# More unread products ahead of TensorE's waits in the two feed-forward layers and in retention's input projections

## The chip, the cores and the metric

The kernel runs on one core of a Trainium2 chip, in one launch. The metric is the device time of one execution in microseconds (us). All arithmetic on the matrices is fp32, with each large product split into three products of rounded fp32 parts (high times high, high times low, low times high), which TensorE takes as `fp32r`, one instruction each. A product of plain fp32 operands stands in the trace as two instructions.

The engines are named as in the profile: PE is TensorE, PEld its loading of weights, DVE VectorE, ACT ScalarE, POOL GpSimd and SP the queue that issues most transfers. Each engine takes its instructions in the order in which the program holds them.

## The reference, cut to what matters

A trunk of two layers works on one sequence of 1024 rows by 1024 columns. Layer 0 mixes with a gated delta rule, layer 1 with retention; each is followed by a convolutional feed-forward network.

```python
for i in range(DEPTH):
    mod = (e @ ada_w[i] + ada_b[i])[:, None, :]
    sh1, sc1, g1, sh2, sc2, g2 = jnp.split(mod, 6, axis=-1)
    y = mixers[i % N_MIXERS](x * (1.0 + sc1) + sh1)
    x = layer_norm(DN_ALPHA * x + (1.0 + g1) * y, ln_g[i, 0], ln_b[i, 0])
    y = conv_ffn(x * (1.0 + sc2) + sh2, ffn_up[i], ffn_conv_w[i], ffn_conv_b[i], ffn_down[i])
    x = layer_norm(DN_ALPHA * x + (1.0 + g2) * y, ln_g[i, 1], ln_b[i, 1])
```

The parts that the change touches are products: the feed-forward network's up projection (1024 to 2 x 2816) and down projection (2816 to 1024), and retention's input projection (1024 to 6144).

```python
gate, up = jnp.split(h @ w_up, 2, axis=-1)          # conv_ffn
return (jax.nn.silu(causal_dwconv(gate, conv_w) + conv_b) * up) @ w_down
q, k, v, gate = jnp.split(h @ w_in, [...], axis=-1)  # retention
```

## The kernel before, in words

**Up projections and retention's input projection** are done by `strassen(...)`. It goes over a list of items; each is two units of 128 output columns. The first two items are plain products. From the third on (`n` = 2, 3, ...) an item is one call of `wino`, a Winograd scheme on a 2 x 2 split: seven block products in place of eight. DVE first adds and subtracts weight blocks (`psub`), ACT and DVE split each sum into a high and a low part (`block`, line 1219 on, whose two instructions are lines 89 and 90), and PE multiplies (`prod`, four times three products, lines 110 to 112; where the product adds to a bank that is in use it goes by `mm_on`, line 1175). In `wino` the products come in the order 11, 12, T1, T2, 22, T3, T4. The product T2 needs the block `w2`, which is the last of a chain on DVE and ACT: `s1`, `s2`, its rounding, its rest.

`strassen` is called three times: for layer 0's feed-forward network, for retention's input projection (with `direct=True`), and for layer 1's feed-forward network.

**Down projections** are done by `proj_gen(...)`, also a Winograd scheme: seven products `p` = 0 to 6, each summed over `nj` pairs of inner blocks (`j`), 11 for the feed-forward network, with four banks of 128 x 512. For each `j`, `ops` loads and splits an activation block (`ab`) and a weight block (`bb`), and PE makes 12 products of 128 x 512 (line 1500). The functions `f1` to `f7` read the banks as each `p` ends. In `p` = 2, two of the four banks come from the pool `sc`, which has two buffers, and two from `acc`, which has four; in `p` = 3 the two `acc` banks come first and the two of `sc` after. `p` = 6 adds to the banks of `p` = 5 after `f7` (line 1475) has read each. `gate` is set for retention's output projection alone, `final` for layer 1's feed-forward network alone.

**Unread products.** `keep_busy(n, mm, behind)` takes a bank from `sc` and issues `n` fp32 products of the identity with 384 columns of constants into it; nothing reads them (line 686). They wait for the bank alone. The kernel before has them at seven places in the code (some through `pm`, which stand in the profile under line 633). Two of these are in `wino` for `n` = 2 without `direct`: three ahead of T1 and three ahead of T2.

**What sets the order.** The instructions are written down in program order, and a scheduler with a model of time then orders each engine's list; `tc.issue_after(x)` keeps an instruction behind `x` in that order. A tile of a pool that is full waits until an older tile of the pool is no longer used, so a bank of `sc` that is asked for while both buffers hold sums cannot be written before one of them was read, wherever it stands in the code.

Of the kernel before, what the change touches and what calls it, by code (L numbers as in the profile page):

```python
# [33 lines left out]
def trunk_kernel(ctx: ExitStack, tc, A):  # L34
    nc = tc.nc
    pe, act, dve, pool, sp = nc.tensor, nc.scalar, nc.vector, nc.gpsimd, nc.sync
# [9 lines left out]
    def tl(tag, shape, dt=F32, name=None):  # L46
        return sb.tile(shape, dt, tag=tag, name=name or tag, bufs=BUFS[tag])
# [10 lines left out]
    def acc_tile():  # L58
        return ps.tile([P, HALF], F32, tag="acc", name="acc", bufs=4)
# [4 lines left out]
    def sc_tile():  # L64
        return ps.tile([P, HALF], F32, tag="sc", name="sc", bufs=2)

    def acc4():
        return [acc_tile(), acc_tile(), acc_tile(), acc_tile()]
# [13 lines left out]
    def hs(half):  # L82
        return slice(half * HALF, (half + 1) * HALF)
# [30 lines left out]
    ended = [None]  # L114
# [509 lines left out]
    def pq(inst, cost):  # L624
        if pin[0] is not None:
            tc.add_manual_dep(inst.ins, pin[0].name,
                              mybir.DependencyInfo(mybir.DependencyClass.NoSync, mybir.DependencyReason.DATA),
                              reason="issue order")
        pin[0] = inst.ins
        clk[0] += cost  # L630

    def pm(out, lhsT, rhs, start=True, stop=True, cost=0.216, **kw):
        r = pe.matmul(out, lhsT, rhs, start=start, stop=stop, **kw)  # L633
        pq(r, cost)
        return r
# [46 lines left out]
    def keep_busy(n, mm, behind=None):  # L682
        t = sc_tile()
        with tc.issue_after(behind) if behind is not None else nullcontext():
            for _ in range(n):
                mm(t[:, 0:3 * P], ident, cst)
# [9 lines left out]
    def take(tag, n):  # L696
        while free[tag] < n:
            yield lambda: free[tag] >= n
        free[tag] -= n

    def give(tag, n):
        free[tag] += n
# [465 lines left out]
    def strassen(hT0, xts, scale, shift, items, tags=("hTb", "hTb", "qkv", "qkv", "aux"), direct=False, beside=None, spare="lane"):  # L1168
# [35 lines left out]
        def bg_steps(n):  # L1204
            for _ in range(0 if n < 4 else 2 if n < 8 else 1):
                bg_step()

        def block(src, it):
            n = nblk[0]
            nblk[0] += 1  # L1210
            t = tl(("wh", "wl")[n % 2], [P, 2, HALF], F32R, name="wb")
            with rank(it):
                split(t[:, 0], t[:, 1], src)
            return kn(t[:, 0]), kn(t[:, 1])

        def prod(it, src, b, onto=None, w=None):
            w = w or block(src, it)
            if onto is None:
                nacc[0] += 1
                acc = (acc_tile, acc_tile, sc_tile)[nacc[0] % 3]()  # L1220
            else:
                acc = onto
            for k in range(4):
                mm3(acc, w, k, B[b][k], onto is None and k == 0, k == 3, mm_on if onto is not None else pe.matmul)
            return acc

        def psub(it, x, y, op=ALU.subtract):
            t = mm_tile()
            with rank(it):
                dve.tensor_tensor(t, x, y, op)  # L1230
            return t

        def wino(n, sink):
            ua, ub = items[n][:2]
            raws = []
            for m, u in ((2 * n, ua), (2 * n + 1, ub)):
                if direct and m % 3 == 0:
                    raws += [tl("xT", [P, HALF], name="wr") for _ in range(2)]
                    for h2 in range(2):
                        anchor["i"] = sp.dma_start(raws[-2 + h2], u[:, hs(h2)])  # L1240
                else:
                    w = tl("wr", [P, D])
                    anchor["i"] = sp.dma_start(w, u)
                    raws += [w[:, hs(0)], w[:, hs(1)]]
            if beside:
                beside(n)
            a11, a12, a21, a22 = raws
            def copy_of(X, tag="cv"):
                t = tl(tag, [P, 516] if tag == "cv" else [P, HALF], name="pc")[:, 0:HALF]
                act.activation(t, X, AF.Copy)  # L1250
                return t

            X = prod(n, a11, "11")
            p1 = copy_of(X)
            s1 = psub(n, a21, a22, ALU.add)
            sink(0, prod(n, a12, "21"), p1)
            s2 = psub(n, s1, a11)
            w1 = block(s1, n)
            if n == 2 and not direct:
                keep_busy(3, pe.matmul, ended[0].ins)  # L1260
            Z = prod(n, None, "T1", w=w1)
            z5 = copy_of(Z)
            s4 = psub(n, a12, s2)
            w2 = block(s2, n)
            if n == 2 and not direct:
                keep_busy(3, pe.matmul, ended[0].ins)
            prod(n, None, "T2", X, w=w2)
            u2 = copy_of(X)
            s3 = psub(n, a11, a21)
            prod(n, s4, "22", Z)  # L1270
            sink(1, Z, u2)
            bg_steps(n)
            prod(n, s3, "T3", X)
            u3 = copy_of(X, "t2")
            sink(3, X, z5)
            sink(2, prod(n, a22, "T4"), u3)
            bg_steps(n if n < 4 else 8)
# [29 lines left out]
    def proj_gen(nj, ablk, wsrc, slots, xsrc, G, final, ln_next, tag, ltags, dst, key, mm=pe.matmul, gate=None, gain=None):  # L1307
# [137 lines left out]
        def finish(half, t, nh, c):  # L1445
            add_row(stats[half][t], nh, xts[half][t][:, hs(nh)], c)
# [51 lines left out]
        for p, (an, bn, fin) in enumerate(prods):  # L1498
            onto = p in (1, 5, 6)
            mm_ = (lambda *a, p=p, onto=onto, **kw: (mm if p < 2 else pe.matmul)(*a, skip_group_check=onto, **kw))  # L1500
            if p in (2, 3):
                accs = [sc_tile(), sc_tile(), acc_tile(), acc_tile()] if p == 2 else [acc_tile(), acc_tile(), sc_tile(), sc_tile()]
            elif not onto:
                accs = acc4()
            tail = []
            depth = ltags[3] if p == 6 else 2
            for j in range(nj):
                if gate and p < 2:
                    yield gate(j)
                    yield from take("qkv", 2)  # L1510
                    give("qkv", 2)
                a, w = ops(p * nj + j)
                ops_ahead(p * nj + j + 1)
                if gate and p == 0 and j == 0:
                    keep_busy(3, lambda *x: pm(*x, cost=0.0))
                if gain and p == 0 and j < 8:
                    gain_half(j)
                if gain and p == 1 and j % 2 == 0 and j < 8:
                    xload(0, j // 2)
                if gate and p == 2 and j < 4:  # L1520
                    xload(0, j)
                if not gate and not gain and p == 2 and j % 2 == 0 and j < 8:
                    xload(0, j // 2)
                if p == 3 and j < 4:
                    finish(0, j, 0, c11[j])
                if j >= nj - depth:
                    tail.append((j, a, w))
                else:
                    for t in range(4):
                        mma(accs[t], t, a, w, j == 0 and not onto, False, mm_)  # L1530
                        yield 0.0
                for _ in range(3 if p == 5 else 1):
                    if later:
                        later.pop(0)()
                if p == 5 and not later:
                    for _ in range(-(-16 // (nj - 4))):
                        if hooks:
                            hooks.pop(0)()
                bg_step()
            while later:  # L1540
                later.pop(0)()
            if p == 5:
                while hooks:
                    hooks.pop(0)()
            if p == 6:
                pin[0] = None
            if p == 6 and final:
                keep_busy(2, pe.matmul, ended[0].ins)
            for t in range(4):
                for j, a, w in tail:  # L1550
                    mma(accs[t], t, a, w, j == 0 and not onto, j == nj - 1,
                        (lambda *x, **kw: pm(*x, skip_group_check=True, **kw)) if p == 6 else mm_)
                fin(t, accs[t])
                yield 0.0
            if p == 1:
                yield "P2"
            if p == 4:
                hooks = [] if final else ln_hooks(0, xts[0], tag, ln_next, outs, dst, key, bal["h"])
                hooks += [lambda t=t: xload(1, t) for t in range(4)]
# [472 lines left out]
```

## Time and profile before

| | |
|---|---|
| time, median of 3 runs | 2918.78 us (2918.34 to 2925.48) |
| the profiled execution | 2926.89 us |
| its span, first to last instruction | 2925.1 us |
| mean granted TensorE clock | 0.994 |
| unread products by line 686 / all instructions of PE | 17 (34 records) / 13718 |

The span is one execution, and it is 6.3 us longer than the median of the three runs. All places below are in us from the start of this span. In the timeline, a row gives the start, the length from the first start to the last end, the engine, line, operation, tiles, shape and count, and in brackets how long the engine had been idle and what ended that. The lengths of PE's instructions overlap, since they are pipelined. The table of stretches gives the busy time of each engine, then `PEclk`, the granted share of TensorE's clock, then the share of the transfer engines and GB/s.

### The profile page before, as it was taken

What the parts mean: (1) busy time and instruction counts of PE and PEld (TensorE: products, weight loads), DVE (VectorE), ACT (ScalarE), POOL (GpSimd) and SP (SyncE); (2) the same over time, 40 slices, a digit from 0 to 9 for tenths busy, and PEclk for the clock granted to TensorE, in tenths of its full rate; (3) what the DMA queues carried; (4) which work ended last, traced back from release to release, by engine and by line L of the source; (5) the groups of instructions that cost most, each with busy time, mean ns of one, the idle gap of its engine ahead of it and who ended that gap; (6) DMA issues with size and microseconds to landing.
All of it is one profiled execution on the core that took longest, in us unless ns stands there. A gap on an engine that the chain in (4) does not pass through costs nothing. (4 is left out here: it accounts for less than half of the span.)

```text
span 2925.1 us, 39004 instructions
## 1 busy us (share of the span) xinstructions
PE 2825.9 (97%) x13718; PEld 2303.7 (79%) x13718; DVE 2204.2 (75%) x3965; ACT 1315.2 (45%) x2457; POOL 423.4 (14%) x485
## 2 busy tenths in 40 slices
PE   8999999999999999999999999999999999999997
PEld 7787877887778878887787877777778788888786
DVE  6695687557788888997687766566797887778878
ACT  3755465443544444536443332221345544444443
POOL 0311220134011111000000000323301011111001
PEclk9999999999999999999999999999999999999999
DMA  8122221354344544863435454555574243335753
GB/s 304 69 80 80 98 91 44 105 189 142 105 155 162 165 159 147 313 220 123 159 108 175 147 186 147 160 158 176 185 243 152 70 164 108 108 108 206 261 155 119
DMA packets 239236, 442.37 MB, mean 151 GB/s; under 512 B 22848, under 2 KB 76352, under 8 KB 239040
## 3 DMA queue, kind: packets, MB, share of 16 engines
q1 hardware_dynamic: 206832, 387.96, 40.1%
q10 hardware_dynamic: 29760, 43.00, 4.0%
q0 software_dynamic: 2448, 8.91, 0.8%
q8 instruction: 108, 1.77, 0.3%
q14 instruction: 88, 0.72, 0.1%
HBM read 331.26 MB, written 108.53 MB: 150 GB/s over the span
## 5 line engine op out<-in xcount | busy, mean ns | idle before, releaser
L1500 PE MATMUL acc<-bb,ab 128*128 128x512 f32 x1800 | 426.0, 392 | 6.5 <-DVE pa L1475 3.3
L1500 PEld LDWEIGHTS acc<-bb,ab 128*128 128x128 f32 x1800 | 337.3, 188 | 80.1 <-issue 3.7
L633 PE MATMUL acc<-hT,wh 128*128 128x512 f32 x960 | 299.8, 394 | 0.0
L1643 POOL TENSOR_TENSOR o<-o 128x512 f32<-128x512 f32 x88 | 121.1, 1385 | 803.1 <-DVE o L1636 753.7
L1175 PE MATMUL acc<-T,wb 128*128 128x512 f32 x840 | 203.0, 391 | 8.1 <-DVE wb L90 7.9
L633 PEld LDWEIGHTS acc<-hT,wh 128*128 128x128 f32 x960 | 182.6, 190 | 34.0
L89 ACT ACTIVATE ab<-ar 128x512 fp32r<-128x512 f32 x210 | 128.7, 623 | 176.0 <-PE acc L1500 72.2
L633 PE MATMUL acc<-hT,wl 128*128 128x512 f32 x480 | 202.4, 422 | 0.8 <-DVE qkv L1008 0.4
L1175 PEld LDWEIGHTS acc<-T,wb 128*128 128x128 f32 x840 | 157.0, 188 | 44.5 <-DVE wb L90 12.2
L90 DVE TENSOR_TENSOR ab<-ar,ab 128x512 fp32r<-128x512 f32 x210 | 147.2, 709 | 42.1 <-ACT ab L89 39.3
L90 DVE TENSOR_TENSOR wb<-mm,wb 128x512 fp32r<-128x512 f32 x216 | 145.4, 686 | 26.8 <-ACT wb L89 25.0
L90 DVE TENSOR_TENSOR wb<-wr,wb 128x512 fp32r<-128x512 f32 x162 | 112.4, 695 | 65.4 <-ACT wb L89 64.7
L89 ACT ACTIVATE wb<-mm 128x512 fp32r<-128x512 f32 x216 | 122.6, 594 | 82.7 <-DVE mm L1230 74.7
L89 ACT ACTIVATE wh<-wr 128x1024 fp32r<-128x1024 f32 x101 | 107.0, 1061 | 116.5 <-PE acc L633 56.0
L90 DVE TENSOR_TENSOR wl<-wr,wh 128x1024 fp32r<-128x1024 f32 x85 | 105.5, 1241 | 62.8 <-ACT wh L89 60.7
L1250 ACT ACTIVATE pc<-acc 128x512 f32<-128x512 f32 x143 | 84.7, 592 | 149.9 <-PE acc L1175 90.8
L89 ACT ACTIVATE wb<-wr 128x512 fp32r<-128x512 f32 x162 | 98.9, 626 | 102.9 <-DMA wr<-in_ffn_up 53.3
L1622 DVE SCALAR_TENSOR_TENSOR o<-g,vc,o 128x512 f32<-128x512 f32 (+2 forms) x176 | 139.1, 808 | 1.5 <-ACT o L1617 0.9
L633 PE MATMUL acc<-wh,hT 128*128 128x512 f32 x384 | 137.0, 419 | 3.2 <-DVE vv L90 3.2
L452 DVE SCALAR_TENSOR_TENSOR qkv<-raw,vc,qkv 128x512 f32<-128x512 f32 x144 | 112.3, 783 | 31.2 <-ACT qkv L450 27.2
L224 DVE SCALAR_TENSOR_TENSOR ada<-mvw,e,ada 128x512 f32<-128x512 f32 x140 | 105.9, 757 | 24.5 <-DMA mvw<-in_ada_w 23.9
L1230 DVE TENSOR_TENSOR mm<-wr 128x512 f32<-128x512 f32 x108 | 79.0, 731 | 53.3 <-DMA wr<-in_ffn_up 30.9
(630 smaller groups left out, 6955.5 us busy)
## 6 DMA issues: line engine op xcount, KB each, us to landing
wr<-in_ffn_up SPq DMA_DIRECT2D x96, 512.0 KB, 4.1
ad<-o SPq DMA_DIRECT2D x154, 256.0 KB, 3.0
ar<-ad SPq DMA_DIRECT2D x154, 256.0 KB, 4.0
mvw<-in_ada_w SPq DMA_DIRECT2D x48, 512.0 KB, 5.2
Br<-in_ffn_down SPq DMA_DIRECT2D x66, 256.0 KB, 3.5
mvw<-in_ada_w SPq DMA_DIRECT2D x64, 256.0 KB, 3.0
wr<-in_ret_wv SPq DMA_DIRECT2D x32, 512.0 KB, 3.7
ar<-od SPq DMA_DIRECT2D x56, 256.0 KB, 5.3
```

Source lines behind the costliest of these rows:

```text
L89: act.activation(dst_h, src, AF.Copy)
L90: eng.tensor_tensor(dst_l, src, dst_h, ALU.subtract)
L224: dve.scalar_tensor_tensor(a, wr[kk], e[:, k:k + 1], a, ALU.mult, ALU.add)
L452: dve.scalar_tensor_tensor(oh, raw[:, 3 - j:515 - j], w[:, 3 - j:4 - j], oh, ALU.mult, ALU.add)
L633: r = pe.matmul(out, lhsT, rhs, start=start, stop=stop, **kw)
L1175: return pe.matmul(*a, skip_group_check=True, **kw)
L1230: dve.tensor_tensor(t, x, y, op)
L1250: act.activation(t, X, AF.Copy)
L1500: mm_ = (lambda *a, p=p, onto=onto, **kw: (mm if p < 2 else pe.matmul)(*a, skip_group_check=onto, **kw))
L1622: dve.scalar_tensor_tensor(tv, gv[:, c0 - j:c1 - j], w[:, 2 - j:3 - j], tv, ALU.mult, ALU.add)
L1643: pool.tensor_tensor(o[d], o[x], o[y], op)
```

## The change

It alters the number of unread products at one place and adds them at three more:

- `wino`, `n` = 2 without `direct` (once in each feed-forward layer), ahead of T2: nine in place of three;
- `wino`, `n` = 4 with `direct` (retention's input projection), ahead of T2: eight, where there were none;
- `proj_gen`, `final`, `p` = 6, `j` = 0 (layer 1's down projection): eight, where there were none;
- `proj_gen` without `gate`, `p` = 2, `j` = 1 (the down projection of both layers): five, where there were none.

That is 38 products of 128 x 384 more, 76 records of PE. No arithmetic that is read changes.

```diff
             if n == 2 and not direct:
-                keep_busy(3, pe.matmul, ended[0].ins)
+                keep_busy(9, pe.matmul, ended[0].ins)
+            if n == 4 and direct:
+                keep_busy(8, pe.matmul, ended[0].ins)
             prod(n, None, "T2", X, w=w2)
...
                 if gate and p == 0 and j == 0:
                     keep_busy(3, lambda *x: pm(*x, cost=0.0))
+                if final and p == 6 and j == 0:
+                    keep_busy(8, pe.matmul, ended[0].ins)
+                if p == 2 and j == 1 and not gate:
+                    keep_busy(5, pe.matmul, ended[0].ins)
```

The order on PE at three places follows. In each, the rows before stand first. `cst` holds the constants, `wb` a split weight block of `wino`, `T_` a block of the activations, `bb` and `ab` the split blocks of `proj_gen`.

Place A, PE in layer 0's up projection, third item: the last product of T1, then T2. Layer 1 has the same.

```order
L112 MATMUL acc<-T_7318,wb 128x512
L686 MATMUL sc<-cst 128x384 x3
L1175 MATMUL acc<-T_7242,wb 128x512 x3
L1175 MATMUL acc<-T_7266,wb 128x512 x3
L1175 MATMUL acc<-T_7290,wb 128x512 x3
L1175 MATMUL acc<-T_7314,wb 128x512 x3
```

```order
L112 MATMUL acc<-T_7318,wb 128x512
L686 MATMUL sc<-cst 128x384 x9
L1175 MATMUL acc<-T_7242,wb 128x512 x3
L1175 MATMUL acc<-T_7266,wb 128x512 x3
L1175 MATMUL acc<-T_7290,wb 128x512 x3
L1175 MATMUL acc<-T_7314,wb 128x512 x3
```

The count alone differs. In retention's input projection the eight new ones stand in the same way between T1 and T2 of the fifth item (place C below).

Place B, PE in layer 0's down projection, with buffer numbers: before, banks 11600 to 11603 are those of `p` = 3, and 11329 to 11332 those of `p` = 2; in the change they are 11612 to 11615 and 11335 to 11338.

```order
L1500 MATMUL acc_11600<-bb_11681,ab_11678 128x512 x3
L1500 MATMUL acc_11601<-bb_11681,ab_11678 128x512 x3
L1500 MATMUL sc_11602<-bb_11566,ab_11563 128x512 [waits DVE_49]
L1500 MATMUL sc_11602<-bb_11566,ab_11563 128x512 x2
L1500 MATMUL sc_11602<-bb_11609,ab_11606 128x512 x3
```

```order
L1502 MATMUL acc_11612<-bb_11693,ab_11690 128x512 x3
L1502 MATMUL acc_11613<-bb_11693,ab_11690 128x512 x3
L686 MATMUL sc_11375<-cst_155 128x384 [waits DVE_49]
L686 MATMUL sc_11375<-cst_155 128x384 x4
L1502 MATMUL sc_11614<-bb_11578,ab_11575 128x512 [waits DVE_49]
L1502 MATMUL sc_11614<-bb_11578,ab_11575 128x512 x2
```

The five products do not stand at `p` = 2, `j` = 1, where the code has them, but after five `j` of `p` = 3 in the `acc` banks and ahead of its first product in an `sc` bank; in layer 1 after four `j`. Between the rows of `j` = 0 and `j` = 1 of `p` = 2 there is nothing new.

Place D, PE in layer 1's down projection, the end of the program:

```order
L1500 MATMUL acc<-bb,ab 128x512 x12
L1500 MATMUL sc<-bb,ab 128x512 x12
L1500 MATMUL acc<-bb,ab 128x512 x324
L686 MATMUL sc<-cst 128x384 x2
L633 MATMUL acc<-bb,ab 128x512 x72
```

```order
L1502 MATMUL acc<-bb,ab 128x512 x12
L1502 MATMUL sc<-bb,ab 128x512 x12
L1502 MATMUL acc<-bb,ab 128x512 x264
L686 MATMUL sc<-cst 128x384 x8
L1502 MATMUL acc<-bb,ab 128x512 x60
L686 MATMUL sc<-cst 128x384 x2
L633 MATMUL acc<-bb,ab 128x512 x72
```

The eight stand ahead of the last 60 products by line 1500, which are the first five `j` of `p` = 6.

On DVE and ACT the scheduler moves single instructions by a few rows near places A, B and C, and near D a split of `ab` goes between two additions of rows; POOL and SP keep their order.

## The prediction

> **What bounds the kernel now.** I read the page first: it says which engine is full.
>
> ```profile
> span 2925.1 us, 39004 instructions
> PE 2825.9 (97%) x13718; PEld 2303.7 (79%) x13718; DVE 2204.2 (75%) x3965; ACT 1315.2 (45%) x2457; POOL 423.4 (14%) x485
> PEclk9999999999999999999999999999999999999999
> ```
>
> PE is busy for 97% of the span, so time that is added to PE's list is added to the span unless it lies in one of PE's own waits. PEclk never shows less than a nine, so little clock is to be won. Next I read PE's timeline for its waits, and stretches of the granted clock around each. The clock changes on a grid of 3.41 us, so I chose stretches of that length on its edges.
>
> The price of one unread product comes from the three ahead of T2 in layer 0 (place A) and the group of line 686.
>
> ```profile
> L686 PE MATMUL sc<-cst x34: 483/486/488, 640.2 to 2894.5; 128*128 128x384 f32 x34
> 806.93 2.10 PE L686 MATMUL sc<-cst 128*128 128x384 f32 x6
> 811.06 3.02 PE L1175 MATMUL acc<-T,wb 128*128 128x512 f32 x12 [2.04 <-DVE wb L90]
> 2312.13 2.10 PE L686 MATMUL sc<-cst 128*128 128x384 f32 x6
> 2316.31 3.02 PE L1175 MATMUL acc<-T,wb 128*128 128x512 f32 x12 [2.08 <-DVE wb L90]
> ```
>
> Six records take 2.10 us and each is 0.486 long, so they start (2.10 - 0.486) / 5 = 0.323 us apart; a product is two records, 0.646 us. The next could start 0.323 after the last start, while the record runs on for 0.486: a wait offers its shown idle time and 0.16 more as room.
>
> **The change part by part.** For each place: products times 0.646, less the room, is the delay; then the clock.
>
> *Place A, twice.* Six more products are 3.88 us. The room is 2.04 + 0.16 = 2.20 and 2.08 + 0.16 = 2.24. The delays are 1.68 and 1.64, together 3.32 us. What PE waited for, the last split of `wb` on DVE, does not depend on the products, so it comes when it came. The clock before was full here (the stretches are below), so this execution has nothing to win back.
>
> *Place B, twice.* The code puts five products at `p` = 2, `j` = 1, where PE waits 1.75 and 1.69 us:
>
> ```profile
> 1259.85 1.65 PE L1500 MATMUL sc<-bb,ab 128*128 128x512 f32 x6 [1.75 <-DVE ab L90]
> 2757.86 1.67 PE L1500 MATMUL sc<-bb,ab 128*128 128x512 f32 x6 [1.69 <-DVE ab L90]
> ```
>
> But both buffers of `sc` hold sums of `p` = 2 then, so PE's order has them some 35 us later, ahead of the first `sc` products of `p` = 3. There the trace has:
>
> ```profile
> 1288.77 5.38 PE L1500 MATMUL acc<-bb,ab 128*128 128x512 f32 x23
> 1293.98 6.96 PE L1500 MATMUL sc<-bb,ab 128*128 128x512 f32 x30
> 2782.52 8.32 PE L1500 MATMUL acc<-bb,ab 128*128 128x512 f32 x36
> 2790.68 5.60 PE L1500 MATMUL sc<-bb,ab 128*128 128x512 f32 x24
> 1289.79 0.72 DVE L1463 TENSOR_TENSOR pa<-sc,pa 128x512 f32<-128x512 f32 x1
> 1291.59 0.72 DVE L1463 TENSOR_TENSOR pa<-sc,pa 128x512 f32<-128x512 f32 x1
> ```
>
> No wait stands ahead of either row of `sc` products: there is no room, and 2 x 5 x 0.646 = 6.46 us go on top. The banks' readers on DVE (line 1463) had ended by 1292.31, ahead of 1293.98, so the bank itself costs no further wait. The old waits of 1.75 and 1.69 stay. Could the delay be swallowed, because DVE sets the pace? DVE is full up to here, but then has slack:
>
> ```profile
> 1304.00:1314.00 10.00, 10.00 (x46) 8.29 (x45) 6.21 (x11) 4.32 (x8) 0.00 (x0) 1.00 0.67 225
> 2802.00:2812.00 10.00, 10.00 (x46) 8.27 (x45) 6.16 (x11) 4.38 (x8) 0.00 (x0) 1.00 0.73 241
> ```
>
> The third number is DVE's busy time: 6.2 of 10 us, with PE at 10 of 10. PE sets the pace, so I take the whole 6.46; the bounds are 0 (swallowed) and 6.46 + 1 (the scheduler moved line 1463's reads by a row on a full DVE, and one instruction there takes 0.72).
>
> *Place C, once.* Eight products are 5.17 us in retention's fifth item.
>
> ```profile
> 1554.26 0.39 PE L112 MATMUL acc<-T,wb 128*128 128x512 f32 x1
> 1557.68 5.49 PE L1175 MATMUL sc<-T,wb 128*128 128x512 f32 x12 [3.03 <-DVE wb L90]
> 1562.97 1.25 PE L1175 MATMUL acc<-22_12947,wb 128*128 128x512 f32 x3
> 1564.75 0.84 PE L1175 MATMUL acc<-22_12987,wb 128*128 128x512 f32 x3
> 1553.58:1556.99 3.41, 1.07 (x5) 0.56 (x3) 3.41 (x7) 2.61 (x5) 0.00 (x0) 1.00 0.22 77
> 1556.99:1560.40 3.41, 2.72 (x6) 2.17 (x7) 3.41 (x7) 0.10 (x1) 1.39 (x2) 0.50 0.60 231
> 1560.40:1563.82 3.42, 3.42 (x10) 2.67 (x8) 0.93 (x2) 1.21 (x3) 0.04 (x1) 0.50 0.91 226
> ```
>
> The room is 3.03 + 0.16 = 3.19, so the delay is 1.98. Here the clock paid: after a stretch in which PE was busy for 1.07 of 3.41 us, two stretches ran at 0.50. Twelve products took 5.49 against 3.02 in the row at 811.06, and three took 1.25 against 0.84: 2.47 + 0.41 = 2.88 us, which go if PE never idles. Net -0.90.
>
> *Place D, once.* Eight products are 5.17 us at the start of `p` = 6 in layer 1.
>
> ```profile
> 2739.70 13.76 PE L1500 MATMUL acc<-bb,ab 128*128 128x512 f32 x60
> 2878.50 15.21 PE L1500 MATMUL acc<-bb,ab 128*128 128x512 f32 x60 [3.34 <-DVE pa L1475]
> 2879.58 1.30 DVE L1475 TENSOR_TENSOR pa<-acc,pa 128x512 f32<-128x512 f32 x2
> 2874.54:2877.95 3.41, 0.62 (x3) 0.19 (x1) 3.41 (x8) 1.65 (x3) 0.93 (x1) 1.00 0.00 0
> 2877.95:2881.37 3.42, 2.87 (x7) 2.32 (x8) 3.42 (x7) 0.00 (x0) 0.36 (x1) 0.50 0.40 153
> ```
>
> The room is 3.34 + 0.16 = 3.50 and the delay 1.67. The half clock up to 2881.37 made 60 products take 15.21 where 60 elsewhere take 13.76: 1.45 us come back. The next two banks are read by 2880.88, before PE would now reach them. Net +0.22. What follows to the end is a chain on DVE behind PE's last products, and shifts with them.
>
> *Given back.* PE that comes later may find a later wait for DVE shorter. After places A these are left:
>
> ```profile
> 1026.77 3.01 PE L1175 MATMUL acc<-T,wb 128*128 128x512 f32 x12 [0.59 <-DVE wb L90]
> 2336.14 2.12 PE L1175 MATMUL sc<-T,wb 128*128 128x512 f32 x8 [0.49 <-DVE wb L90]
> 2400.37 0.50 PE L110 MATMUL sc<-T,wb 128*128 128x512 f32 x1 [0.47 <-DVE wb L90]
> ```
>
> Together 1.55 us at most, nothing at least, since DVE there also waits for PE's banks; I take 0.6.
>
> *The sum.* Delays 3.32 + 6.46 + 1.98 + 1.67 = 13.43; clock 2.88 + 1.45 = 4.33; given back 0.6: +8.5 us. The profiled execution took 2926.89 us (a span of 2925.1 and 1.8 around it), so it would take 2935.4. It lies 8.1 above the median of the runs; the profile doesn't show why, so I add the difference, not a ratio, to the median: 2918.78 + 8.5 = 2927.3 us. A measurement of this kernel can tell about 0.3% from no change, which is 8.8 us: the forecast lies on that edge.
>
> *A rule against the trace.* How long must a wait be to cost clock?
>
> ```profile
> 1990.37 1.57 PE L633 MATMUL sc<-vv,kz 128*128 128x512 f32 x3 [2.08 <-DVE on L1862]
> 1987.08:1990.49 3.41, 1.33 (x7) 0.79 (x6) 3.25 (x6) 0.00 (x0) 1.46 (x1) 1.00 0.84 241
> 1990.49:1993.90 3.41, 3.41 (x14) 3.13 (x15) 2.43 (x4) 0.47 (x1) 0.00 (x0) 0.50 0.97 333
> 2311.32:2314.74 3.42, 2.91 (x11) 1.60 (x9) 3.42 (x6) 2.41 (x5) 0.00 (x0) 1.00 0.20 77
> 2314.74:2318.15 3.41, 1.84 (x8) 1.54 (x9) 3.41 (x7) 1.62 (x3) 0.00 (x0) 1.00 0.01 2
> ```
>
> A wait of 2.08 us that lay wholly in one stretch of the grid halved the clock of the next; layer 1's wait at place A, also 2.08, was split by the edge at 2314.74 and cost nothing. So with the grid elsewhere, A's waits cost clock too. The Trainium skill, page "TensorE: Matmul & The Clock Gate", section "Why this matters for your kernels", warns only of idle gaps of more than about 3 us. By that rule nine products at A could never pay, and the sum would stay at 13.43 - 4.33 = 9.1 less what is given back, in every execution. By the rows, an execution whose grid catches A's two waits whole loses up to 1.5 us at each before the change (as at D, 1.45), and the sum falls to about 5.5. The rows decide.
>
> **The rivals.**
>
> *Not slower: DVE absorbs the down projections' delay.* If the cover at B is there after all, B's 6.46 and D's 1.67 are gone, and 3.32 + 1.98 - 4.33 - 0.6 = +0.4 is left: 2919.2. For it: DVE is full from 1294 to 1304. Against it: the slack after 1304 and 2802. It decides from the point where the waits after B shorten by over 3 us in each layer; no such waits stand there. To be faster by 0.3%, A's clock would have to come back as well, and more. Chance 0.15.
>
> *Smaller: the grid lies so that A's waits cost clock before.* 8.5 - 3.0 = +5.5, 2924.3. For it: the wait at 1990.37. Against it: neither did here. Chance 0.2.
>
> *Larger: the clock isn't won.* If the runs' grid spared C and D before, or the clock falls at another wait now, 13.43 - 0.6 = +12.8, 2931.6. For it: half clock depends on the grid. Against it: C's room of 3.19 and D's of 3.50 nearly fill a stretch of 3.41, and are hard to split harmlessly. Chance 0.15.
>
> **How the numbers follow.** The forecast itself has 0.5: 2927.3 us. The cases run from 2919.2 to 2931.6; the runs before lie from 0.4 below to 6.7 above their median. With that on the upper side, and B's bound of 1, I give 2919.5 to 2936. Slower by over 0.3% (above 2927.5): half of the forecast's 0.5, nearly all of the larger case and a little of the others for the scatter, some 0.48. Within 0.3%: the rest but for 0.07, the part of the absorbing case in which A's clock and the scatter add to it.
>
> **What would show it.** In the profile after: PE's list has runs of 18, 16, 16 and 10 records of line 686; the waits ahead of T2 in the three items and ahead of `p` = 6 are gone; the waits of 1.75 and 1.69 at `p` = 2, `j` = 1 are still there, with ten records some 35 us behind them and PE without a wait before and after; the clock is full behind places C and D, and the row of 60 products at the end takes about 13.8. I am wrong if the ten records at B stand where PE idled, if the waits behind them shrink, or if the stretches at half clock are fewer at places that the change doesn't touch.

## The result, and the profile after

| | before | after |
|---|---|---|
| median of five runs on one chip, us | 2921.93 | 2938.38 |
| lowest and highest, us | 2918.34 to 2925.48 | 2934.19 to 2939.32 |
| profiled execution, us | 2926.89 | 2938.46 |
| its span, us | 2925.1 | 2936.6 |
| mean granted clock | 0.994 | 0.995 |

The ratio of after to before is 1.0055, with a 95% interval of 1.0043 to 1.0068: slower by about 16 us (12.6 to 19.9). The side was forecast rightly. The size was not: 8.5 us were forecast, and 2938.38 lies above the range's upper end, 2936.

The page of the profile after, first part:

```profile
span 2936.6 us, 39160 instructions
PE 2845.5 (97%) x13794; PEld 2313.3 (79%) x13794; DVE 2200.5 (75%) x3965; ACT 1315.0 (45%) x2457; POOL 422.4 (14%) x485
```

PE has 76 instructions more, and its busy time grew by 19.6 us while the span grew by 11.5. The busy times of DVE, ACT and POOL moved by less than 4 us. So the time is on PE's list, and the question is which of the added products stand in a wait and which do not.

PE's timeline of the profile after answers that. Each row has start, duration, the products and, in brackets, the idle time ahead of it. The places follow in order: A of layer 0, B of layer 0 (first the old wait, then the new products), C, the two items after C, A of layer 1, B of layer 1, D.

```profile
803.90 5.97 PE L686 MATMUL sc<-cst 128*128 128x384 f32 x18
809.41 3.23 PE L1175 MATMUL acc<-T,wb 128*128 128x512 f32 x12
...
1259.72 1.67 PE L1502 MATMUL sc<-bb,ab 128*128 128x512 f32 x6 [1.75 <-DVE ab L90]
1284.38 9.68 PE L1502 MATMUL acc<-bb,ab 128*128 128x512 f32 x42
1293.90 3.39 PE L686 MATMUL sc<-cst 128*128 128x384 f32 x10
1296.83 3.91 PE L1502 MATMUL sc<-bb,ab 128*128 128x512 f32 x15
...
1518.81 5.32 PE L686 MATMUL sc<-cst 128*128 128x384 f32 x16
1523.67 3.19 PE L1175 MATMUL acc<-T,wb 128*128 128x512 f32 x12
1543.79 3.04 PE L1175 MATMUL acc<-T,wb 128*128 128x512 f32 x12 [0.60 <-DVE wb L90]
1567.51 4.46 PE L1175 MATMUL sc<-T,wb 128*128 128x512 f32 x12 [3.58 <-DVE wb L90]
...
2318.26 5.97 PE L686 MATMUL sc<-cst 128*128 128x384 f32 x18
2799.64 3.39 PE L686 MATMUL sc<-cst 128*128 128x384 f32 x10
2802.56 3.23 PE L1502 MATMUL sc<-bb,ab 128*128 128x512 f32 x12
2887.23 5.32 PE L686 MATMUL sc<-cst 128*128 128x384 f32 x16
2892.09 14.07 PE L1502 MATMUL acc<-bb,ab 128*128 128x512 f32 x60
```

A, B and D look as forecast: the waits at A and D are gone, the wait of 1.75 us at `p` = 2, `j` = 1 is still there, and the ten records of B stand in a full list 34 us behind it. C does not. The prediction said that the wait of 3.03 us, ahead of twelve products `sc<-T,wb`, would be filled. The eight products stand at 1518.81, and that wait, now 3.58 us, stands at 1567.51, two items further on. Twelve products of one T2 stand between them, at 1543.79. The stretch in which that wait ends still runs at half clock (the columns are those of the prediction, the clock is the third from the end):

```profile
1563.79:1567.20 3.41, 0.14 (x1) 0.00 (x0) 3.41 (x7) 2.33 (x5) 0.05 (x1) 1.00 0.23 77
1567.20:1570.61 3.41, 3.10 (x7) 2.48 (x8) 3.27 (x6) 0.00 (x0) 1.38 (x2) 0.50 0.60 231
1570.61:1574.02 3.41, 3.41 (x16) 2.77 (x15) 0.89 (x2) 1.60 (x3) 0.00 (x0) 1.00 0.89 237
```

The timeline of before shows what the prediction overlooked. The rows are the T2 of the fifth item and that of the sixth; the T2 that the prediction took for the fifth's is the seventh's:

```profile
1515.50 2.88 PE L1175 MATMUL acc<-T,wb 128*128 128x512 f32 x12
...
1535.31 3.02 PE L1175 MATMUL acc<-T,wb 128*128 128x512 f32 x12 [0.61 <-DVE wb L90]
```

The row at 1515.50 has no idle time ahead of it. C had no room at all. From it to the sixth item's T2 are 19.81 us before; from the start of the eight products to the sixth item's T2 are 1543.79 - 1518.81 = 24.98 us after. The difference is 5.17, which is 8 x 0.646 to the last digit.

To price every place in this way I compared the times of the same read product in the two traces: the **local shift** of a place is how much later PE is behind it, less how much later it was ahead of it. It is much sharper than a median, since it leaves out what varies elsewhere.

| place | forecast, us | local shift after, us |
|---|---|---|
| A, layer 0 and layer 1 | 1.68 + 1.64 | 1.55 + 1.54 |
| B, layer 0 and layer 1 | 3.23 + 3.23 | 3.27 + 3.27 |
| C | -0.90 | 5.17 |
| D | 0.22 | 0.23 |
| sum | 9.1 | 15.0 |

My theory then: the change costs 15 us, and the whole miss is C, whose wait was located in the wrong item. The rival theory: C's local cost is taken back at DVE's next wait, and the excess comes from A, B and D, which shift DVE's and ACT's work on a PE that is never far ahead of them.

### The profile page after: what moved, and what is told of

Read it like the earlier page. It is cut to its first block, busy times and chain, and to the rows that moved or that the text cites. A ratio compares the mean times of both kernels' runs of the same rounds, so it can differ in the third digit from the quotient of the medians.

```text
span 2936.6 us, 39160 instructions
## 1 busy us (share of the span) xinstructions
PE 2845.5 (97%) x13794; PEld 2313.3 (79%) x13794; DVE 2200.5 (75%) x3965; ACT 1315.0 (45%) x2457; POOL 422.4 (14%) x485
```

## The experiments

Every kernel was run in five rounds beside the kernel before. Ratios are to before, with 95% intervals. "Only" means that one line of the change is put into the kernel before.

**A alone** (`e1_only_a`).

```diff
-                keep_busy(3, pe.matmul, ended[0].ins)
+                keep_busy(9, pe.matmul, ended[0].ins)
```

> Nine products ahead of T2 in place of three, in both feed-forward layers, and nothing else of the change. Theory of places (a product costs 0.646 us of PE wherever PE does not wait, and only what fits into a wait is free): 12 x 0.646 less the rooms of 2.20 and 2.24 = +3.3 us, of which some is won back where the clock fell here before. Theory of order (the surplus of the change over the forecast comes from DVE's and ACT's changed rows around the third item): +5 to +7 us, with new waits for wb behind the third item. If the extra products pay by the clock: 0 or below.

Measured: 2923.95 us, ratio 1.0018 (1.0006 to 1.0029), some 5 us (1.8 to 8.5). The local shifts are 1.59 and 1.58. The forecast's +3.3 lies in the interval.

**B alone** (`e2_only_b`).

```diff
+                if p == 2 and j == 1 and not gate:
+                    keep_busy(5, pe.matmul, ended[0].ins)
```

> Five products at p = 2, j = 1 of both down projections, which the order puts at the first sc bank of p = 3, and nothing else of the change. Theory of places: no wait there, so 10 x 0.646 = +6.5 us, with the old waits of 1.75 and 1.69 us unchanged. Rival (DVE sets the pace of the down projections and swallows PE's delay): +0 to +2 us.

Measured: 2928.88 us, ratio 1.0028 (1.0016 to 1.0040), some 8 us (4.7 to 11.7). The local shift is 3.27 in each layer, and the waits of 1.75 and 1.69 us are still there. PE's timeline of this kernel, first around A of layer 0, then around B:

```profile
802.94 2.10 PE L686 MATMUL sc<-cst 128*128 128x384 f32 x6
807.07 4.60 PE L1175 MATMUL acc<-T,wb 128*128 128x512 f32 x12 [2.04 <-DVE wb L90]
...
1291.90 3.39 PE L686 MATMUL sc<-cst 128*128 128x384 f32 x10
1294.83 3.91 PE L1500 MATMUL sc<-bb,ab 128*128 128x512 f32 x15
```

At B no wait stands ahead of the ten records or behind them, so five products cost five products; DVE absorbs nothing. At A, which this kernel leaves alone, the same twelve products that took 3.02 us in the profile of before took 4.60 here. The stretches tell why:

```profile
803.81:807.22 3.41, 1.38 (x5) 0.53 (x4) 3.41 (x7) 3.35 (x6) 0.00 (x0) 1.00 0.20 77
807.22:810.63 3.41, 3.41 (x9) 2.64 (x10) 2.80 (x5) 0.01 (x1) 1.14 (x1) 0.50 0.28 108
```

The wait of 2.04 us lies whole in one stretch, and the next runs at 0.50. That is the mechanism of the rival "smaller", and its price is 4.60 - 3.02 = 1.58 us.

**C alone** (`e3_only_c`).

```diff
+            if n == 4 and direct:
+                keep_busy(8, pe.matmul, ended[0].ins)
```

> Eight products ahead of T2 in the fifth item of retention's input projection, and nothing else of the change. Theory of places, with the place read anew in the profile after (the products stand near 1519, where PE did not wait before; the wait of 3.03 us at 1554.65 is that of the seventh item): 8 x 0.646 = +5.2 us, the wait of about 3 us some 40 us behind the products stays, and so does the half clock behind it. The forecast's reading (the products lie in that wait): -0.9 us.

Measured: 2928.86 us, ratio 1.0028 (1.0017 to 1.0038), some 8 us (5.0 to 11.1); the local shift is 5.17. The forecast's -0.90 lies outside. PE's timeline of this kernel shows the same picture as the profile after, with nothing else changed:

```profile
1517.05 5.32 PE L686 MATMUL sc<-cst 128*128 128x384 f32 x16
1521.92 3.19 PE L1175 MATMUL acc<-T,wb 128*128 128x512 f32 x12
...
1564.36 4.23 PE L1175 MATMUL sc<-T,wb 128*128 128x512 f32 x12 [2.99 <-DVE wb L90]
```

The products push PE 5.17 us back, and the wait two items on has 2.99 us where it had 3.03: DVE, whose splits PE waits for there, is held up as much as PE is, so nothing is given back.

**D alone** (`e4_only_d`).

```diff
+                if final and p == 6 and j == 0:
+                    keep_busy(8, pe.matmul, ended[0].ins)
```

> Eight products at the start of p = 6 in layer 1, and nothing else of the change. Theory of places: 8 x 0.646 - 3.50 = +1.7 us on PE, of which 1.4 come back where the half clock behind the wait is gone: +0.2 us, the same within what can be measured. Rival (the end is set by DVE, which does not move): 0.

Measured: 2920.38 us, ratio 0.9996 (0.9986 to 1.0005); the local shift is 0.23, against a forecast of 0.22. In this pair of profiles delay and clock cancel.

**C's products put where the wait is** (`e5_c_moved`): the eight go ahead of T2 of the seventh item.

```diff
+            if n == 6 and direct:
+                keep_busy(8, pe.matmul, ended[0].ins)
```

> The same eight products as in e3, moved from the fifth to the seventh item of retention's input projection, ahead of T2, where the kernel before waits 3.03 us; nothing else of the change. Theory of places: delay 8 x 0.646 - 3.19 = +2.0 us, less the half clock behind that wait (2.9 us where it cost two stretches, 1.4 where one): 0 +- 1 us, some 5 us below e3. Rival (the eight products cost 5.2 us wherever they stand, since DVE's wait only moves behind them): +5.2, as e3.

Measured: 2923.52 us, ratio 1.0014 (1.0005 to 1.0023), some 4 us (1.5 to 6.7). That is above what was expected. PE's timeline of this kernel at the place, however, is what the forecast had wanted of C:

```profile
1556.62 5.32 PE L686 MATMUL sc<-cst 128*128 128x384 f32 x16
1561.49 3.19 PE L1175 MATMUL sc<-T,wb 128*128 128x512 f32 x12
1564.52 0.84 PE L1175 MATMUL acc<-22_12947,wb 128*128 128x512 f32 x3
```

The wait is gone, twelve products take 3.19 in place of 5.49, three 0.84 in place of 1.25, and the local shift is -1.0 against the forecast's -0.90. The term was computed rightly for a wait that belonged to another item. It holds for the profile of before, though, and not for most executions: of the ten profiles that keep this wait, three lost two stretches to half clock, as the forecast assumed, and seven lost one. On average these ten pass the place 0.9 us earlier than the profile of before does, so against them the eight products win about nothing. Why the median lies some 4 us above before all the same is not settled: in the profiled execution both of A's waits, which this kernel leaves alone, cost clock (1.6 us each against the profile of before), and between 2870 and 2910 us it lost another 3 us; whether its other executions do so more often than those of before cannot be seen.

**B's products put where the wait is** (`e6_b_in_wait`): three, in a bank of another pool that is free at `p` = 2, `j` = 1, so that nothing holds them back.

```diff
-    def keep_busy(n, mm, behind=None):
-        t = sc_tile()
+    def keep_busy(n, mm, behind=None, tile=sc_tile):
+        t = tile()
...
+                if p == 2 and j == 1 and not gate:
+                    keep_busy(3, pe.matmul, ended[0].ins, mm_tile)
```

> Three products at p = 2, j = 1 of both down projections with a bank of the pool mm in place of sc, so that the order keeps them in the wait of 1.75 and 1.69 us; nothing else of the change. Theory of places: 3 x 0.646 = 1.94 against rooms of 1.91 and 1.85: +0.1 us, the same, and no wait at those two rows any more. Rival (products in the down projection cost their own time wherever they stand): 6 x 0.646 = +3.9 us.

Measured: 2922.79 us, ratio 1.0007 (0.9997 to 1.0018). PE's timeline of this kernel:

```profile
1254.81 2.10 PE L686 MATMUL mm<-cst 128*128 128x384 f32 x6
1256.72 1.66 PE L1500 MATMUL sc<-bb,ab 128*128 128x512 f32 x6
```

Three products of 1.94 us stand in the wait of 1.75 (and 0.16 more), no idle time is left, and the local shift is 0.00. The wait did not cost clock before, so filling it wins nothing either. The bank is what had moved B's five products 34 us on.

**The change without C** (`e8_change_without_c`): A, B and D as in the change.

> The whole change but for the eight products in retention's fifth item. Theory of places: +3.3 (third items) + 6.5 (p = 3) + 0.2 (p = 6), less up to 3 for half clock at the third items: +8 to +10 us over the kernel before, about 5 us below the change. Rival (the places act on each other through the changed rows of DVE, and the surplus is not that of the fifth item): +13 to +16, as the change.

Measured: 2929.06 us, ratio 1.0024 (1.0014 to 1.0033), some 7 us (4.1 to 9.6), where the whole change took 1.0055 (1.0043 to 1.0068). The intervals do not touch. The local shifts of A, B and D are 1.59, 3.27, 1.58, 3.27 and 0.23, as in the change. So the rival theory falls: without C the rest costs what the forecast gave it (3.32 + 6.46 + 0.22 - 0.6 = 9.4 lies inside).

**C doubled** (`e9_c_double`): 16 products at `n` = 4 in the kernel before.

```diff
+            if n == 4 and direct:
+                keep_busy(16, pe.matmul, ended[0].ins)
```

> Sixteen products in place of eight in retention's fifth item, and nothing else of the change. Theory of places (nothing hides them, so the price is linear): 16 x 0.646 = +10.3 us, 5.2 more than e3. Rival (e3's surplus is DVE's changed rows, not the products): about e3's +8 again.

Measured: 2932.90 us, ratio 1.0042 (1.0029 to 1.0055), some 12 us (8.5 to 16); the local shift is 10.33, twice 5.17. PE's timeline of this kernel:

```profile
1509.55 10.48 PE L686 MATMUL sc<-cst 128*128 128x384 f32 x32
1519.58 3.19 PE L1175 MATMUL acc<-T,wb 128*128 128x512 f32 x12
```

Had there been a wait somewhere ahead or DVE slack to swallow a part, the second eight would have cost another amount than the first. They cost the same.

**The three products at A left out** (`e10_none_at_t2`): the line `keep_busy(3, ...)` ahead of T2 goes.

> The three products ahead of T2 in the third items, which the kernel before already has, are left out; nothing else is changed. Theory of places: the waits there grow from 2.04 and 2.08 to about 3.98 us and the end of each wait stays where it was, so no PE time is won; each wait now costs half clock in nearly every execution, 1.5 to 3 us each where before it did in some 4 of 10: +2 to +4 us. Rival (waits at the third item do not matter for the clock, or unread products don't pay): 0 or below.

Measured: 2923.76 us, ratio 1.0011 (0.9999 to 1.0022). PE's timeline of this kernel:

```profile
808.14 4.57 PE L1175 MATMUL acc<-T,wb 128*128 128x512 f32 x12 [3.97 <-DVE wb L90]
```

The wait grows by what was taken out (2.04 + 1.94 = 3.98), the clock falls, and the twelve products take 4.57. The local shifts are 1.61 and 2.23 in the two layers: against the profile of before, in which these waits cost no clock, the three products are worth having. The interval, which takes in no change, doesn't show it by itself.

**As many products as each wait has room for** (`e7_fit`, and the same kernel once more as `e11_fit_again`): six at A, four at the seventh item, five at D, two in the free bank at B, with `keep_busy` taking the pool as it did for B's three.

```diff
-                keep_busy(3, pe.matmul, ended[0].ins)
+                keep_busy(6, pe.matmul, ended[0].ins)
+            if n == 6 and direct:
+                keep_busy(4, pe.matmul, ended[0].ins)
...
+                if final and p == 6 and j == 0:
+                    keep_busy(5, pe.matmul, ended[0].ins)
+                if p == 2 and j == 1 and not gate:
+                    keep_busy(2, pe.matmul, ended[0].ins, mm_tile)
```

> Products cut to fit the waits: six ahead of T2 in the third item of both feed-forward layers, four in retention's seventh item in place of eight in the fifth, five at p = 6 of layer 1, two (in a bank of mm) at p = 2, j = 1 of both down projections. Theory of places: every delay is 0 or below, and the half clock behind these waits is gone: -2.9 (seventh item, two stretches) or -1.4, -1.4 (p = 6), and up to -1.5 at each of the third items in executions where the clock falls there: -3 to -6 us, faster by 0.1 to 0.2%. Rival (unread products never win more than they cost): 0 or slower.

> The kernel of e7 once more, since its interval held both no change and the expected gain. Theory of places: -3 to -6 us, of which the interval should now exclude a loss of more than 1 us. Rival (cut to fit, they win nothing that lasts): 0.

Measured: 2918.14 us, ratio 0.9995 (0.9984 to 1.0006), then 2918.35 us, ratio 0.9990 (0.9980 to 0.9999): some 1.5 and 2.9 us faster, less than was expected, and the first interval takes in no change. PE's timeline of the first, at the seventh item and at D:

```profile
1554.03 2.74 PE L686 MATMUL sc<-cst 128*128 128x384 f32 x8
1557.08 3.01 PE L1175 MATMUL sc<-T,wb 128*128 128x512 f32 x12 [0.31 <-DVE wb L90]
...
2867.27 3.39 PE L686 MATMUL sc<-cst 128*128 128x384 f32 x10
2870.19 14.11 PE L1502 MATMUL acc<-bb,ab 128*128 128x512 f32 x60
```

At A the local shifts are 0.01 to 0.03 in both profiles, at the seventh item -3.0 and -3.17, at D -1.67: the delays are nil and the clock comes back. The stretch of 100 us around the seventh item, in the profile of before and then in the first of the fitted kernel:

```profile
1500.00:1600.00 100.00, 95.75 (x408) 78.14 (x407) 79.20 (x130) 35.09 (x62) 4.29 (x6) 0.97 0.46 158
...
1500.00:1600.00 100.00, 98.01 (x427) 79.58 (x426) 81.58 (x133) 35.35 (x64) 5.00 (x7) 1.00 0.49 166
```

From 700 to 2900 us each of the 22 such stretches of the fitted kernel has 1.00, in both profiles; in the profile of before four have 0.97 or 0.98. So as many unread products as the waits have room for clearly beat the change. They beat before by about 0.1% at most, which only the second series shows by itself, and just so.

## Why the prediction was right or wrong

**The failed step is C.** The prediction read the wait of 3.03 us at 1557.68 as that of retention's fifth item. It belongs to the seventh. The code says `n == 4`, and the trace doesn't number items: each T2 is a row of twelve products by line 1175 ahead of four rows of three, one in some 20 us, and the prediction gives no count of them for its choice. Counted from the third item, or read by its neighbours, 1515.50 is the fifth. The term should have been +5.17 with no clock won. The miss of C is 5.17 + 0.90 = 6.1 us; 8.5 + 6.1 = 14.6, which the measured 12.6 to 19.9 holds. That the wait and the half clock two items later stay was shown by C alone, that the rest costs no more than forecast by the change without C, and that C's price is plain PE time by the doubling.

The baseline added to the miss, and that is chance: the forecast stood on the median of the first three runs, 2918.78, and the median of the five is 2921.93, so 3.15 of the 11.1 us between 2927.3 and 2938.38 are the baseline's. On the old baseline the right sum of 14.6 would have given 2933.4, inside the range.

**The price of a product** was right to two digits: 5.17 for eight, 10.33 for sixteen, 3.27 for five.

**A** was right in the profiled pair, 1.55 and 1.54 against 1.68 and 1.64. By that difference the room is some 0.1 more than idle time plus 0.16; why isn't shown.

**B** was right in size and in place: the order, not the code, said where the products stand, and no wait there gave them cover. The rival in which DVE absorbs them falls by B alone.

**D** was right to 0.01 us in the profiled pair, and no profile with D has its wait. That the figure fits so well is luck: the profile of before has the longest wait at D of the eight profiles that don't fill it (2.10 to 3.34 us), and half clock followed in only four of these. PE's timeline with A alone has a wait of 2.28 and no clock lost there, and PE waits for DVE soon after:

```profile
2873.01 13.85 PE L1500 MATMUL acc<-bb,ab 128*128 128x512 f32 x60 [2.28 <-DVE pa L1475]
...
2893.30 13.21 PE L633 MATMUL acc<-bb,ab 128*128 128x512 f32 x57 [1.69 <-DVE ab L90]
```

Its local shift at D is -2.41. Counted from the last product ahead of the wait to the end of the span, though, it is only 0.14 us shorter than before. The fitted kernel's -1.67 at D is likewise only -0.49 and -0.40 at the end of the span, in its two profiles. So what PE wins or loses at D doesn't all reach the end, where the prediction had the chain on DVE shift with PE's last products; what holds DVE there wasn't tried.

**Given back: 0.6 was taken, none is seen.** The waits of 0.59 us at 1026.77 and 0.49 us at 2336.14 have no counterpart after, but the first is missing in five and the second in nine of the eleven other profiles too, kernels without A among them. In their place PE's timeline of the profile after has these, the first three in layer 0's up projection, the fourth in layer 1's, two in layer 1's down projection:

```profile
947.21 3.02 PE L1175 MATMUL sc<-T,wb 128*128 128x512 f32 x12 [0.48 <-DVE wb L90]
...
1065.25 3.01 PE L1175 MATMUL sc<-T,wb 128*128 128x512 f32 x12 [0.80 <-DVE wb L90]
...
1105.02 2.34 PE L1175 MATMUL acc<-T,wb 128*128 128x512 f32 x9 [0.47 <-DVE wb L90]
...
2407.52 0.50 PE L110 MATMUL sc<-T,wb 128*128 128x512 f32 x1 [0.64 <-DVE wb L90]
...
2725.70 5.31 PE L1502 MATMUL acc<-bb,ab 128*128 128x512 f32 x21 [0.73 <-DVE ab L90]
2732.19 8.04 PE L1502 MATMUL acc<-bb,ab 128*128 128x512 f32 x34 [1.18 <-ACT pa L1457]
```

Waits of this size come and go between executions; the local shift from 830 to 1150 us is 1.29 here, and -0.35 with A alone, -0.84 with D alone and 3.37 with C alone, which touches nothing there. A wait of half a microsecond in one profile is no fund to draw on.

**The rivals.** "Smaller" has its mechanism shown, and oftener than its chance of 0.2 said: in the profiles of the seven kernels that keep three products at A (before among them), the clock fell behind A in 3 of 7 executions in layer 0 and in 4 of 7 in layer 1. It costs about 1.6 us each time, just what nine products' delay costs, so over many executions A's price should be nearer to half of 3.3. The runs don't settle it: A alone (1.8 to 8.5) speaks for the whole price, the change without C (4.1 to 9.6, where the local shifts add to 9.9) for less. It could not show in the balance, since C's 6.1 went the other way. "Larger" came near in size (12.8) for another reason: the clock was not won at C because the products were not at that wait.

**What stays open.** The profiled pair differs by 11.5 us and its local shifts add to 15.0. The profile of before holds more at places that the change doesn't touch: 2.3 us between 640 and 800, which the prediction's offset of 8.1 us had hinted at, and 3.0 us between 1700 and 1990. The first is that execution's own, since eleven of the twelve other profiles lie 1.8 to 2.5 us below it there. Of the second, 1.5 us lie at 1855, where before lost a stretch to half clock (from 1857.37) and the profile after didn't. The prediction had named such a stretch, gone at a place that the change doesn't touch, as a sign of being wrong. But it comes and goes without the change: four profiles have it (before, B alone, C alone and B's three in the free bank), and nine lack it, among them that of D alone, which changes nothing ahead of place D. Nor is it settled why the medians of the kernels with A, B or C alone lie 1.6 to 3 us above their local shifts. The shifts lie in the measured intervals, except that of the eight products at the seventh item and, by 0.3 us, the sum without C.

## What to carry to other kernels

Before a wait is priced as room for an edit, make sure that it is the edit's own: count the items from a landmark in the trace, and match the rows on both sides of the edit in the instruction order with rows on both sides of the wait. Work that only fills time costs nothing inside a wait and its full duration a row outside it, and the buffer that it takes may move it out. Size it by the idle time and not beyond: 2.04 us of wait held three products more at no cost and six more cost 1.6 us. And read a wait in more than one execution before it is priced: D's was anything from 2.10 to 3.34 us.

## What the runs showed of the hardware

**How much idle time halves the clock.** In the eleven profiles whose clock changes between 700 and 2900 us (all but the two of the fitted kernel) I laid the grid of 3.41 us over PE's idle time, from 650 to 2900 us. At full clock, 36 stretches held 1.9 us of idle time or more, and 34 of them were followed by one at 0.50; the two others held 1.91 and 1.92. Of 29 stretches with 1.3 to 1.8 us, 28 were followed by full clock and one (1.69) by half. So the edge lies near 1.9 us of idle time in one stretch, and a wait of 2.04 us is on the costly side if the grid doesn't split it, while B's waits of 1.75 are just on the free side. The Trainium skill, page "TensorE: Matmul & The Clock Gate", section "Why this matters for your kernels", warns of idle gaps over about 3 us; the runs here show that much shorter ones cost clock.

**Full clock throughout is worth little here.** With the products fitted to the waits, no stretch from 700 to 2900 us ran below full clock in either profile, and the kernel gained about 1.5 to 3 us of 2920.
